# Two attention heads' scores strictly in turns, their values in fp32 on 64-column halves, and ln1_g loaded in one tile with x

## The chip, the cores and the metric

One core of one Trainium2 chip runs the kernel. The metric is the device time of one execution in microseconds (us). The kernel before took 611.07 us (median of 3 runs, 610.78 to 611.39).

## What is computed

One layer of a hybrid decoder on 256 tokens of width 1024, all in float32. The reference, cut to what the change touches:

```python
h  = rms_norm(x, ln1_g)
q, k, v, z, xbc, dt_raw, gate_a, gate_b = split(h @ w_in, IN_OFFSETS)
qh = rms_norm(split_heads(q), q_norm_g)          # 16 heads of 64
kh = rms_norm(split_heads(k), k_norm_g)
s_own = where(kpos <= qpos, qh @ kh.T * 64 ** -0.5, -inf)
att   = softmax(s_own) @ split_heads(v)
y_a = att @ w_o_attn
y_b = mamba2_mixer(z, xbc, dt_raw, ...) @ w_o_ssm
x = x + (sigmoid(gate_a) * y_a + sigmoid(gate_b) * y_b) @ w_out
x = x + SwiGLU(rms_norm(x)) ;  x = x + (p @ w_ple_proj) * sigmoid(rms_norm(x) @ w_ple_gate)
```

With 256 tokens there is one block, so attention is plain causal attention.

## The kernel before

Every large product runs as 128x512 matmuls with activations as weights (one tile of 128 tokens) and the weight matrix as the moving side. To keep float32 accuracy at the speed of the one-pass type fp32r, each operand is split into a rounded high part and the low rest, and three products are summed: high x high, high x low, low x high (`mm3`, L169; `Panel.step`, L319). The weights come from HBM on SP's queue in pieces (`raw`); ScalarE (ACT) rounds a piece (`wh`), VectorE (DVE) subtracts (`wl`) in `split_w` (L230). 2256 of these big matmuls run one after another, in an order that dependencies fix (`queue`, L154: each instruction of TensorE (PE) follows the last big one recorded before it).

Everything else on PE is a small unit between two big matmuls: transposes (L175), the state-space products, attention. These are generators that a small planner (`Filler`, L78) resumes after each big matmul's three products; `fill.now` counts PE's time by a cost per matmul (L167), and the table `LAG` (L68) says how long after one step a task's next may be placed. The framework's scheduler then orders the units that lie behind the same big matmul, and may put some big ones between the members of a unit.

Attention (`attention_task`, L721) takes eight pairs of heads; a pair's 128 features lie on the 128 partitions, one head on each half. `scores` (L725) runs `mm3` for the first head, twice (128 queries on 128 keys, then 128 on 256), and then for the second: twelve fp32r matmuls with 64 rows, into one PSUM tile a head. DVE adds the mask and takes the maximum (L739, L742), ACT exponentiates, DVE normalises (L755). `transp` (L759) transposes the probabilities, six times, and ACT and DVE split them into `h0, l0, h1, l1`. `values` (L777) multiplies v's high and low parts, 128 columns that hold both heads, by both heads' probabilities in six matmuls of 512 and 256 columns; half of each product (one head's v with the other's probabilities) is not used, and the rest is copied out a head at a time (L791, L792). A matmul on fp32 operands, as `transpose` and the state-space `out_` (L637) have it, is two records in the trace.

The start: `load_first` (L250) issues g1 (ln1_g) and x's first tile on ACT's queue and the weight pieces of the first two panels on SP's; `split_h` (L292) multiplies x by g1 on ACT and makes the low part on DVE. Nine matmuls on zeros run before them (L187).

Of the kernel before, what the change touches and what calls it, by code (L numbers as in the profile page):

```python
# [16 lines left out]
P = 128  # L17
T = 256
# [50 lines left out]
    "dt": 9538, "dt.t": 3583, "dt.e": 24762, "dt.low": 1745, "dt.end": 5569, "xbc": 3815, "xbc.t": 1612,  # L69
    "xbc.end": 7699, "z": 8310, "z.t": 1286, "z.end": 1974, "qk": 14749, "qk.t": 2429, "qk.end": 663,  # L70
    "v": 3190, "cb": 436, "rows": 3738, "prep": 3559, "seg": 921, "seg.next": 7841, "out": 9793,
    "out.xdt": 3087, "out.end": 0, "off": 4613, "off.end": 0, "finish": 6096, "finish.ones": 2544, "sc": 857,
    "sc.tr": 2402, "tr": 822, "tr.val": 5876, "val": 3318, "val.end": 8813, "m": 5271, "res": 4539, "ff": 232,
    "ff.end": 5364,
# [34 lines left out]
def tile_layer(ctx: ExitStack, tc: tile.TileContext, xt, xk, pt, vec, w_dt, w_big, w_dn2, w_pp, out):  # L109
# [34 lines left out]

    def bcast(ap2, n):
        return ap2.unsqueeze(2).to_broadcast([ap2.shape[0], ap2.shape[1], n])
# [7 lines left out]
    def queue(ins, main):  # L154


        if fill.last is not None:
            tc.add_manual_dep(
                ins, fill.last.name, mybir.DependencyInfo(mybir.DependencyClass.NoSync, mybir.DependencyReason.DATA),
                reason="order of the tensor engine")  # L160
        if main:
            fill.last = ins

    def mm(o, lhsT, rhs, start, stop, main=False):
        queue(nc.tensor.matmul(o, lhsT, rhs, start=start, stop=stop).ins, main)  # L165
        passes = 4 if lhsT.dtype == F32 else 1
        fill.now += passes * max(107.0, rhs.free_size() / 2.4)  # L167

# [10 lines left out]
    with prio("w"):  # L179
# [7 lines left out]
        for _ in range(9):  # L187
            nc.tensor.matmul(pw[:, :P], zero, zero, start=True, stop=True)
# [31 lines left out]
    def load_x(k, n, queue=nc.sync):  # L220
        queue.dma_start(xraw[k // 2][:, k % 2 : k % 2 + n], xt[:, k : k + n])
# [70 lines left out]
    def split_h(k):  # L292
        g = g1[:, k : k + 1]
        xk_ = xraw[k // 2][:, k % 2]
# [156 lines left out]
    xsT, zsT, bc, qk_t, v_hl, gates = {}, {}, {}, {}, {}, {}  # L451
# [90 lines left out]
    def evac_v(i, pan):  # L542
        vh = s4([2, 512], F32R)
        vl = s4([2, 512], F32R)
        with prio("ev"):
            for tt in range(2):
                act(vh[:, tt], pan.ps[tt], scale=rstd1[:, tt : tt + 1])
                stt(vl[:, tt], pan.ps[tt], rstd1[:, tt : tt + 1], vh[:, tt].bitcast(F32), op0=ALU.mult, op1=ALU.subtract)
        yield fill.now + LAG["v"]
        v_hl[i] = (vh, vl)  # L550
# [13 lines left out]
    def ssm_task():  # L564
# [72 lines left out]
        def out_(g, qd):  # L637
# [3 lines left out]
            with prio("bg"):  # L641
                yds = [pb([2, P]) for _ in range(2)]

                for j in range(2):
                    for c in range(2):
                        for hf in range(2):
                            r0 = slice(64 * hf, 64 * hf + 64)
                            c0 = (2 * qd + j) * P + 64 * hf
                            mm(yds[j][r0, c], xdt[:, c, c0 : c0 + 64], ms[g, qd, c][:, 2 * j + hf], True, True)
# [71 lines left out]
    def attention_task():  # L721
# [3 lines left out]
        def scores(p):  # L725
            half, i = p
            (qh, ql), (kh, kl) = qk_t["q", half], qk_t["k", half]
            with prio("bg"):
                mx = tiny([4])
                sm = tiny([4])  # L730
                sc = []
                s_all = s4([2, 384])
                for hf in range(2):
                    r = slice(64 * hf, 64 * hf + 64)
                    p_ = pb([512])
                    mm3(p_[:, 0:P], qh[r, i, 0:P], ql[r, i, 0:P], kh[r, i, 0:P], kl[r, i, 0:P])
                    mm3(p_[:, P : P + T], qh[r, i, P:T], ql[r, i, P:T], kh[r, i], kl[r, i])
                    s_ = s_all[:, hf]
                    nc.vector.tensor_tensor_reduce(  # L739
                        out=s_[:, 0:P], in0=p_[:, 0:P], in1=cmask[:, 1], scale=1.0, scalar=-3.0e38,  # L740
                        op0=ALU.add, op1=ALU.max, accum_out=mx[:, 2 * hf : 2 * hf + 1])
                    nc.vector.tensor_tensor_reduce(  # L742
                        out=s_[:, P : P + T], in0=p_[:, P : P + T], in1=cmask.rearrange("p a b -> p (a b)"), scale=1.0, scalar=-3.0e38,
                        op0=ALU.add, op1=ALU.max, accum_out=mx[:, 2 * hf + 1 : 2 * hf + 2])
                    sc.append(s_)
                nc.vector.tensor_scalar(mx, mx, -0.125, None, op0=ALU.mult)  # L746
                for hf in range(2):
                    for qt, sl in ((0, slice(0, P)), (1, slice(P, P + T))):
                        n = 2 * hf + qt
                        act(sc[hf][:, sl], sc[hf][:, sl], AF.Exp, scale=0.125, bias=mx[:, n : n + 1], accum_out=sm[:, n : n + 1])  # L750
                nc.vector.reciprocal(sm, sm)
                for hf in range(2):
                    for qt, sl in ((0, slice(0, P)), (1, slice(P, P + T))):
                        n = 2 * hf + qt
                        nc.vector.tensor_scalar(sc[hf][:, sl], sc[hf][:, sl], sm[:, n : n + 1], None, op0=ALU.mult)  # L755
            sc_of[p] = sc
            tm["s", p] = fill.now

        def transp(p):  # L759
            sc = sc_of.pop(p)  # L760
            with prio("bg"):
                p0 = pb([2, T])
                p1 = pb([2, P])
                for hf in range(2):
                    transpose(p0[:, hf, 0:P], sc[hf][:, 0:P])
                    transpose(p0[:, hf, P:T], sc[hf][:, P:T])
                    transpose(p1[:, hf], sc[hf][:, T : T + P])
                hi, lo = s4([6, P], F32R), s4([6, P], F32R)
# [317 lines left out]
```

## Time and profile before

| | us |
|---|---|
| median of 3 runs | 611.07 |
| the profiled execution | 612.0 |
| its span, first to last instruction | 610.2 |
| PE busy | 601.2 (2949 records) |
| DVE busy | 437.8 |
| ACT busy | 341.9 |
| POOL busy | 40.2 |

Busy time of PE is that of overlapping records, so the start of one matmul to the start of the next says more than a record's own length. The mean granted clock of TensorE is given as 0.998 of full rate.

### The profile page before, as it was taken

To read this page: it belongs to the slowest core of one execution; us is meant where nothing else is said; L and a number is where in the kernel's file an instruction comes from. 1 tells how busy PE (TensorE), PEld (TensorE's weight loads), DVE (VectorE), ACT (ScalarE), POOL (GpSimd) and SP (SyncE) were. 2 spreads that over 40 slices of the span, in tenths; PEclk is the share of its full clock that TensorE was granted. 3 is DMA by queue.
4 is the path that set the end of the run, shared out by engine and by line. 5 is a ranking of instruction groups with operands and counts; after the bars stand their busy time and mean duration, and the time that the engine had idled before them with its cause. 6 is when DMAs were issued, how large, how long until landed. Compare 5 with 4: busy or idle time off the path is not lost.

```text
span 610.2 us, 8184 instructions
## 1 busy us (share of the span) xinstructions
PE 601.2 (99%) x2949; PEld 493.1 (81%) x2949; DVE 437.8 (72%) x715; ACT 341.9 (56%) x524; POOL 40.2 (7%) x47
## 2 busy tenths in 40 slices
PE   7999999999999999999999999999999999999997
PEld 6888888777787878888788888888888888888886
DVE  3579999988798774778897576657666666546465
ACT  3676766656584445567647544755544544435353
POOL 2000102331101200102000000000000000000000
PEclk9999999999999999999999999999999999999999
DMA  8755554453435445554444466555556555565641
GB/s 250 259 198 173 182 159 139 145 169 110 139 111 166 156 155 168 168 184 154 139 124 153 146 212 229 172 183 189 180 180 200 173 188 192 176 197 180 195 150 69
DMA packets 31192, 103.88 MB, mean 170 GB/s; under 512 B 3696, under 2 KB 4784, under 8 KB 31152
## 3 DMA queue, kind: packets, MB, share of 16 engines
q1 hardware_dynamic: 30864, 103.23, 52.6%
q8 instruction: 23, 0.38, 0.3%
q10 hardware_dynamic: 288, 0.14, 0.2%
q14 instruction: 17, 0.14, 0.1%
HBM read 102.23 MB, written 1.05 MB: 169 GB/s over the span
## 4 chain that ended last, share of the span: by engine, by line
PE 97%; DMA 1%; DVE 1%; ACT 0%; issue 0%; ACTq 0%
PE g L165 84%; PE pb L165 7%; PE pb L175 5%; DMA xraw<-in_xt 1%; DVE s L474 0%; ACT wh L149 0%; DVE wl L233 0%; ACT s L149 0%; DVE s L526 0%; DVE tiny L522 0%; DVE s L1019 0%; DVE s L1020 0%; ACTq L254 0%; DVE tiny L523 0%; ACT L149 0%
## 5 line engine op out<-in xcount | busy, mean ns | idle before, releaser
L165 PE MATMUL g<-wh,s 128*128 128x512 f32 x1504 | 488.4, 396 | 2.9 <-ACT wh L149 2.9
L165 PEld LDWEIGHTS g<-wh,s 128*128 128x128 f32 x1504 | 283.0, 189 | 62.0 <-ACT wh L149 3.2
L233 DVE TENSOR_TENSOR wl<-raw,wh 128x1024 fp32r<-128x1024 f32 (+1 forms) x192 | 229.8, 1201 | 117.3 <-ACT wh L149 114.8
L165 PE MATMUL g<-wl,s 128*128 128x512 f32 x752 | 295.9, 393 | 0.0
L149 ACT ACTIVATE wh<-raw 128x1024 fp32r<-128x1024 f32 (+1 forms) x192 | 199.4, 1042 | 167.1 <-PE g L165 145.7
L165 PEld LDWEIGHTS g<-wl,s 128*128 128x128 f32 x752 | 142.2, 189 | 27.9 <-DVE wl L233 0.6
L149 ACT ACTIVATE s<-pb 128x512 f32<-128x512 f32 (+5 forms) x76 | 37.2, 505 | 33.9 <-PE pb L175 24.3
L175 PEld LDWEIGHTS pb<-ident,s 128*128 128x128 f32 x302 | 37.8, 140 | 11.5 <-issue 1.2
L175 PE MATMUL pb<-ident,s 128*128 128x128 f32 x302 | 46.7, 272 | 0.0
L149 ACT ACTIVATE s<-g,rstd 128x512 f32<-128x512 f32 (+2 forms) x50 | 28.5, 583 | 22.4 <-PE g L165 21.8
L165 PE MATMUL pb<-s,s 128*64 128x128 f32 (+7 forms) x312 | 39.5, 304 | 0.6 <-DVE s L474 0.6
L165 PEld LDWEIGHTS pb<-s,s 128*64 128x64 f32 (+3 forms) x312 | 30.4, 163 | 9.0 <-issue 4.1
L474 DVE SCALAR_TENSOR_TENSOR s<-pb,vecs,s 128x255 f32<-128x255 f32 (+2 forms) x72 | 32.1, 474 | 1.3 <-ACT s L149 1.1
L149 ACT ACTIVATE s<-pb,vecs 128x256 f32<-128x256 f32 (+2 forms) x48 | 26.0, 552 | 11.8 <-PE pb L175 7.4
L149 ACT ACTIVATE s<-s 128x512 f32<-128x512 f32 (+3 forms) x24 | 19.1, 795 | 8.4 <-DVE s L934 4.0
L335 POOL TENSOR_TENSOR rstd<-tiny,mhalf 128x2 f32<-128x2 f32 x3 | 2.3, 763 | 325.8 <-DVE tiny L334 299.4
L591 POOL TENSOR_SCALAR_AFFINE_SELECT rr<-a_h 128x512 fp32r<-128x512 f32 x16 | 14.3, 902 | 104.3 <-PE pb L165 66.8
L525 POOL TENSOR_TENSOR tiny<-tiny,mhalf 128x8 f32<-128x8 f32 x8 | 15.7, 1966 | 61.1 <-ACT s L149 31.5
L149 ACT ACTIVATE s<-s,tiny 128x128 f32<-128x128 f32 (+1 forms) x32 | 14.1, 446 | 7.0 <-DVE tiny L746 7.0
L978 DVE SCALAR_TENSOR_TENSOR s<-g,rstd,s 128x256 f32<-128x256 f32 x22 | 10.6, 481 | 7.4 <-ACT s L149 7.3
L632 DVE TENSOR_TENSOR s<-s,s 128x512 f32<-128x512 f32 x16 | 11.5, 722 | 0.0
L979 DVE SCALAR_TENSOR_TENSOR s<-g,rstd,s 128x256 f32<-128x256 f32 x22 | 10.6, 484 | 0.8
(121 smaller groups left out, 253.8 us busy)
## 6 DMA issues: line engine op xcount, KB each, us to landing
raw<-in_w_big SPq DMA_DIRECT2D x180, 512.0 KB
raw<-in_w_big SPq DMA_DIRECT2D x8, 256.0 KB
s<-in_xk SPq DMA_DIRECT2D x4, 512.0 KB
raw<-in_w_pp SPq DMA_DIRECT2D x2, 512.0 KB
raw<-in_w_dn SPq DMA_DIRECT2D x2, 512.0 KB
out<-s SPq DMA_DIRECT2D x3, 256.0 KB
xraw<-in_xt SPq DMA_DIRECT2D x2, 256.0 KB
xraw<-in_xt SPq DMA_DIRECT2D x3, 128.0 KB
```

The costliest lines, as they stand in the source:

```text
L149: return nc.scalar.activation(o, i, f, **kw)
L165: queue(nc.tensor.matmul(o, lhsT, rhs, start=start, stop=stop).ins, main)
L175: queue(nc.tensor.transpose(o, i, ident[: i.shape[0], : i.shape[0]]).ins, False)
L233: nc.vector.tensor_sub(wl, raw, wh.bitcast(F32))
L335: nc.gpsimd.tensor_tensor(dst, t, mhalf[:, : ss.shape[-1]], op=ALU.pow)
L474: stt(cc[:, sft:], pu[:, j, : T - sft], cw[3 - sft], cc[:, sft:], op0=ALU.mult, op1=ALU.add)
L525: nc.gpsimd.tensor_tensor(f, ms, mhalf, op=ALU.pow)
L591: nc.gpsimd.affine_select(r, bcast(a_h[:, c, h0 : h0 + 4].bitcast(F32), P), pattern=[[0, 4], [1, P]], compare_op=ALU.is_ge, fill=0.0, base ...
L632: nc.vector.tensor_tensor(m, m, cbm[:, g, c].unsqueeze(1).to_broadcast([P, 4, P]), op=ALU.mult)
L978: stt(t[:, tt], pan.ps[tt][:, :T], r, t[:, tt], op0=ALU.mult, op1=ALU.mult)
L979: stt(t[:, tt], pan.ps[tt][:, T:], r, t[:, tt], op0=ALU.mult, op1=ALU.mult)
```

## The change

- `scores`: the twelve matmuls alternate strictly between the two heads; a new helper, `halves`, chains them so that the scheduler keeps that order. The state-space `out_` is written with the same helper. The normalisation is two broadcast multiplications in place of four.
- `evac_v`, `transp`, `values`: v and the transposed probabilities stay fp32 (no low parts). `values` serves two pairs at a time, in one PSUM tile: each head's product has its own 64 columns of weights and is an fp32 matmul; the heads alternate; one copy on ACT and one subtraction on DVE for both pairs.
- The start: g1 and x's first tile are one array in HBM and one DMA, `x0`, first on SP's queue; seven matmuls on zeros in place of nine.
- The `LAG` table has other numbers, which moves units between other big matmuls.

```diff
 LAG = {
-    "dt": 9538, "dt.t": 3583, "dt.e": 24762, "dt.low": 1745, "dt.end": 5569, "xbc": 3815, "xbc.t": 1612,
+    "dt": 9198, "dt.t": 3823, "dt.e": 24762, "dt.low": 2074, "dt.end": 6965, "xbc": 3815, "xbc.t": 1507,
...
+    def halves(products):
+
+        last = None
+        for a in products:
+            ins = mm(*a)
+            fill.now -= 53.0
+            if last is not None:
+                follow(ins, last)
+            last = ins
...
-        for _ in range(9):
+        for _ in range(7):
...
-    g1 = const.tile([P, 8], F32, name="g1")
+
+    x0 = const.tile([P, 8 + T], F32, name="x0")
+    g1 = x0[:, 0:8]
...
-            nc.scalar.dma_start(g1, vec[:, V_G1 : V_G1 + 8])
-            load_x(0, 1, nc.scalar)
+            nc.sync.dma_start(x0, xt[:, : 8 + T])
...
-        vh = s4([2, 512], F32R)
-        vl = s4([2, 512], F32R)
+        vt = s4([2, 512])
         with prio("ev"):
             for tt in range(2):
-                act(vh[:, tt], pan.ps[tt], scale=rstd1[:, tt : tt + 1])
-                stt(vl[:, tt], pan.ps[tt], rstd1[:, tt : tt + 1], vh[:, tt].bitcast(F32), op0=ALU.mult, op1=ALU.subtract)
+                act(vt[:, tt], pan.ps[tt], scale=rstd1[:, tt : tt + 1])
...
-                    mm3(p_[:, 0:P], qh[r, i, 0:P], ql[r, i, 0:P], kh[r, i, 0:P], kl[r, i, 0:P])
-                    mm3(p_[:, P : P + T], qh[r, i, P:T], ql[r, i, P:T], kh[r, i], kl[r, i])
...
+                halves(
+                    (ps[hf][:, o], a[rows_of[hf], i, qs], b[rows_of[hf], i, ks], n == 0, n == 2)
+                    for o, qs, ks in ((slice(0, P), slice(0, P), slice(0, P)), (slice(P, P + T), slice(P, T), slice(0, T)))
+                    for n, (a, b) in enumerate(((qh, kh), (qh, kl), (ql, kh)))
+                    for hf in range(2))
...
-                act(h0, p0)
-                nc.vector.tensor_sub(l0, p0, h0.bitcast(F32))
-                act(h1, p1)
-                nc.vector.tensor_sub(l1, p1, h1.bitcast(F32))
...
+                act(t0, p0)
+                act(t1, p1)
...
-                mm3(pa, vh[:, 0, cs], vl[:, 0, cs], h0, l0, stop=False)
-                mm3(pa[:, :, P:T], vh[:, 1, cs], vl[:, 1, cs], h1, l1, start=False)
-                for hf in range(2):
-                    r = slice(64 * hf, 64 * hf + 64)
-                    act(ah[r, i], pa[r, hf])
-                    nc.vector.tensor_sub(al[r, i], pa[r, hf], ah[r, i].bitcast(F32))
+                prods = []
+                for i in range(2):
+                    t0, t1 = pr_of.pop((half, i0 + i))
+                    cols = [slice((i0 + i) * P + 64 * hf, (i0 + i) * P + 64 * hf + 64) for hf in range(2)]
+                    prods += [(pa[rows_of[hf], i], vt[:, 0, cols[hf]], t0[:, hf], True, False) for hf in range(2)]
+                    prods += [(pa[rows_of[hf], i, P:T], vt[:, 1, cols[hf]], t1[:, hf], False, True) for hf in range(2)]
+                halves(prods)
+                act(ah, pa)
+                nc.vector.tensor_sub(al, pa, ah.bitcast(F32))
```

A unit of scores on PE before (pb_1532 and pb_1541 are the two heads' PSUM tiles, in each row the moving operand stands first, then the weights: s_188 and s_189 are k's high and low parts, s_222 and s_223 q's):

```order
L165 MATMUL pb_1532<-s_188_1053,s_222_1182 128x128
L165 MATMUL pb_1532<-s_189_1054,s_222_1182 128x128
L165 MATMUL pb_1532<-s_188_1053,s_223_1183 128x128
L165 MATMUL pb_1532<-s_188_1053,s_222_1182 128x256
L165 MATMUL pb_1532<-s_189_1054,s_222_1182 128x256
L165 MATMUL pb_1532<-s_188_1053,s_223_1183 128x256
L165 MATMUL pb_1541<-s_188_1053,s_222_1182 128x128
L165 MATMUL pb_1541<-s_189_1054,s_222_1182 128x128
L165 MATMUL pb_1541<-s_188_1053,s_223_1183 128x128
L165 MATMUL pb_1541<-s_188_1053,s_222_1182 128x256
L165 MATMUL pb_1541<-s_189_1054,s_222_1182 128x256
L165 MATMUL pb_1541<-s_188_1053,s_223_1183 128x256
```

and such a unit in the change, with the heads' tiles pb_1692 and pb_1693:

```order
L170 MATMUL pb_1692<-s_188_1050,s_220_1174 128x128
L170 MATMUL pb_1693<-s_188_1050,s_220_1174 128x128
L170 MATMUL pb_1692<-s_189_1051,s_220_1174 128x128
L170 MATMUL pb_1693<-s_189_1051,s_220_1174 128x128
L170 MATMUL pb_1692<-s_188_1050,s_221_1175 128x128
L170 MATMUL pb_1693<-s_188_1050,s_221_1175 128x128
L170 MATMUL pb_1692<-s_188_1050,s_220_1174 128x256
L170 MATMUL pb_1693<-s_188_1050,s_220_1174 128x256
L170 MATMUL pb_1692<-s_189_1051,s_220_1174 128x256
L170 MATMUL pb_1693<-s_189_1051,s_220_1174 128x256
L170 MATMUL pb_1692<-s_188_1050,s_221_1175 128x256
L170 MATMUL pb_1693<-s_188_1050,s_221_1175 128x256
```

The same twelve products now alternate. Before, six of the eight units stood whole and two had big matmuls between the heads; in the change six stand whole and two have big matmuls after the first of the twelve.

The end of attention on PE before (pb_3409 holds the last pair's values, s_695 and s_696 are the high and low parts of its probabilities, s_583 and s_584 those of v, g_3420 and g_3421 the output projection's panel):

```order
L165 MATMUL pb_3409<-s_695_3372,s_583_2805 128x512
L165 MATMUL g_3421<-wl_3424,s_571_2737 128x512
L165 MATMUL g_3421<-wh_3423,s_572_2738 128x512
L165 MATMUL pb_3409<-s_696_3373,s_583_2805 128x512
L165 MATMUL pb_3409<-s_695_3372,s_584_2806 128x512
L165 MATMUL pb_3409<-s_695_3372,s_583_2805 128x2x128
L165 MATMUL pb_3409<-s_696_3373,s_583_2805 128x2x128
L165 MATMUL pb_3409<-s_695_3372,s_584_2806 128x2x128
L165 MATMUL g_3421<-wh_3423,s_571_2737 128x512
```

and in the change (pb_3316 holds the last two pairs' values, s_687 the last pair's probabilities, s_583 v, both fp32; s_678 and s_679 are the high and low parts that ACT and DVE make of them, the weights of the panel's second half; x2 is the two heads in turn):

```order
L170 MATMUL pb_3316<-s_687_3313,s_583_2796 64x256 x2
L170 MATMUL pb_3316<-s_687_3313,s_583_2796 64x128 x2
L170 MATMUL g_3328<-wh_3336,s_577_2766 128x512
L170 MATMUL g_3327<-wh_3366,s_678_3269 128x512
L170 MATMUL g_3327<-wl_3367,s_678_3269 128x512
L170 MATMUL g_3327<-wh_3366,s_679_3270 128x512
L170 MATMUL g_3327<-wh_3366,s_678_3269 128x512
L170 MATMUL g_3327<-wl_3367,s_678_3269 128x512
L170 MATMUL g_3327<-wh_3366,s_679_3270 128x512
L170 MATMUL g_3327<-wh_3372,s_678_3269 128x512
L170 MATMUL g_3327<-wl_3373,s_678_3269 128x512
L170 MATMUL g_3327<-wh_3372,s_679_3270 128x512
```

The first two rows are the last half of the last values unit, which the order has split; its first half stands 23 big matmuls earlier. Six big matmuls of the second half use features that are long there; the seventh to ninth (wh_3372, the third k step) use those of the last two pairs. Before, the last pair's values stood 15 big matmuls ahead of the panel's second half; now one does.

The start, on ACT before:

```order
L254 DMA g_110<-in_vec 128x8
L149 ACT_TABLE_LOAD
L149 ACTIVATE warm<-warm 128x1
L221 DMA xraw_111<-in_xt 128x256
L149 ACTIVATE s_7_115<-xraw_111,g_110 128x256
L149 ACTIVATE wh_122<-raw_121 128x512
L149 ACTIVATE wh_125<-raw_124 128x512
```

and on SP in the change:

```order
L273 DMA x_108<-in_xt 128x264
L280 DMA raw_118<-in_w_big 128x512
L280 DMA raw_121<-in_w_big 128x512
L240 DMA xraw_109<-in_xt 128x256
L280 DMA raw_118<-in_w_big 128x512
L280 DMA raw_121<-in_w_big 128x512
```

ACT's two DMAs are gone; x and g1 stand ahead of the weight pieces on SP's queue, which were first before.

## Rows read from the trace of the kernel before

**Rows 1.** The page, part 4: the chain that ended last, by engine.
```profile
PE 97%; DMA 1%; DVE 1%; ACT 0%; issue 0%; ACTq 0%
```
**Rows 2.** Timeline of the start, one chain piece among it: start us, length us, what.
```profile
0.80 0.87 SPq L262 DMA_DIRECT2D raw<-in_w_big  x2
1.14 4.21 PE L188 MATMUL pb<-zero 128*128 128x128 f32 x18 [1.14 <-DVE ones L192]
1.29 5.75 DMA xraw<-in_xt
7.13 0.51 ACT L149 ACTIVATE s<-xraw,g 128x256 fp32r<-128x256 f32 x1 [4.40 <-DMA xraw<-in_xt]
8.21 0.80 PE L165 MATMUL g<-wh,s 128*128 128x512 f32 x1 [2.86 <-ACT wh L149]
8.98 1.14 ACT L149 ACTIVATE wh<-raw 128x512 fp32r<-128x512 f32 x2
```
**Rows 3.** Stretches of 2 us: busy us by engine, clock, DMA share, GB/s.
```profile
2.00:4.00 2.00, 2.00 (x11) 2.00 (x11) 0.00 (x0) 0.72 (x2) 1.94 (x8) 1.00 0.87 227
4.00:6.00 2.00, 1.35 (x7) 1.05 (x5) 0.00 (x0) 0.00 (x0) 0.17 (x1) 1.00 0.83 139
```
**Rows 4.** Timeline of PE around 14 us; between two of these rows lie three steps.
```profile
12.94 0.63 PE L165 MATMUL g<-wl,s 128*128 128x512 f32 x1
...
14.20 0.39 PE L165 MATMUL g<-wl,s 128*128 128x512 f32 x1
...
14.90 0.39 PE L165 MATMUL g<-wl,s 128*128 128x512 f32 x1
```
**Rows 5.** Timeline of PE: a whole unit of scores between big matmuls.
```profile
148.28 0.39 PE L165 MATMUL g<-wh,s 128*128 128x512 f32 x1
148.60 1.24 PE L165 MATMUL pb<-s,s 64*128 64x128 f32 x12
149.77 0.50 PE L165 MATMUL g<-wh,s 128*128 128x512 f32 x1
150.11 0.39 PE L165 MATMUL g<-wl,s 128*128 128x512 f32 x1
```
**Rows 6.** Timeline of PE: one head's half of a unit that was split.
```profile
292.22 0.39 PE L165 MATMUL g<-wh,s 128*128 128x512 f32 x1
292.53 0.95 PE L165 MATMUL pb<-s,s 64*128 64x128 f32 x6
293.42 0.50 PE L165 MATMUL g<-wh,s 128*128 128x512 f32 x1
```
**Rows 7.** Timeline of PE: half of a state-space output unit, and a whole one.
```profile
123.18 0.66 PE L165 MATMUL pb<-s,s 128*64 128x128 f32 x8
123.77 0.50 PE L165 MATMUL g<-wl,s 128*128 128x512 f32 x1
...
145.00 0.39 PE L165 MATMUL g<-wh,s 128*128 128x512 f32 x1
145.31 1.09 PE L165 MATMUL pb<-s,s 128*64 128x128 f32 x16
146.34 0.50 PE L165 MATMUL g<-wh,s 128*128 128x512 f32 x1
```
**Rows 8.** Timeline of PE: a unit of values.
```profile
311.10 0.39 PE L165 MATMUL g<-wh,s 128*128 128x512 f32 x1
311.33 1.20 PE L165 MATMUL pb<-s,s 128*128 128x512 f32 x6
312.36 0.40 PE L165 MATMUL g<-wh,s 128*128 128x512 f32 x1
```
**Rows 9.** A wait of PE; ACT and DVE on 128x512: lines, and min/median/max ns.
```profile
PE pb L165 <- DVE s L474: 0.6, 1, 0.6
...
L149 ACT ACTIVATE s<-pb 128x512 f32<-128x512 f32 (+5 forms) x76 | 37.2, 505 | 33.9 <-PE pb L175 24.3
...
L914 DVE TENSOR_TENSOR s<-s,s x4: 682/684/691, 353.0 to 369.5; 128x512 f32<-128x512 f32 x4
```

More of the change, by code (lines that the diff above doesn't have):

```diff
@@ L157, in queue, with follow @@
         if fill.last is not None:
-            tc.add_manual_dep(
-                ins, fill.last.name, mybir.DependencyInfo(mybir.DependencyClass.NoSync, mybir.DependencyReason.DATA),
-                reason="order of the tensor engine")
+            follow(ins, fill.last)
         if main:
             fill.last = ins
+    def follow(ins, before):
+        tc.add_manual_dep(
+            ins, before.name, mybir.DependencyInfo(mybir.DependencyClass.NoSync, mybir.DependencyReason.DATA),
+            reason="order of the tensor engine")
     def mm(o, lhsT, rhs, start, stop, main=False):
-        queue(nc.tensor.matmul(o, lhsT, rhs, start=start, stop=stop).ins, main)
+        ins = nc.tensor.matmul(o, lhsT, rhs, start=start, stop=stop).ins
+        queue(ins, main)
         passes = 4 if lhsT.dtype == F32 else 1
         fill.now += passes * max(107.0, rhs.free_size() / 2.4)
+        return ins
+    def halves(products):
[6 more added lines that the diff above has]
+            last = ins
     def mm3(o, lh, ll, rh, rl, start=True, stop=True):
@@ L293, in split_h @@
         g = g1[:, k : k + 1]
[L294 removed]
+        xk_ = xraw[k // 2][:, k % 2] if k else x0[:, 8:]
         tc.keep_in_program_order(act(h_act[k][0], xk_, scale=g))
@@ L751, in scores @@
                 nc.vector.reciprocal(sm, sm)
[L752 to L756, printed above, removed]
+                for qt, sl in enumerate(parts):
+                    nc.vector.tensor_tensor(
+                        s[:, :, sl], s[:, :, sl], bcast(sm.rearrange("p (h q) -> p h q", h=2)[:, :, qt], sl.stop - sl.start), op=ALU.mult)
@@ L775, in transp, with values @@
+            pr_of[p] = (t0, t1)
             tm["t", p] = fill.now
-        def values(p):
-            half, i = p
-            vh, vl = v_hl[half]
-            if i == 0:
+        def values(half, i0):
+            vt = v_of[half]
+            if i0 == 0:
                 att_hl[half] = (s4([4, T], F32R), s4([4, T], F32R))
-            ah, al = att_hl[half]
-            h0, l0, h1, l1 = pr_of.pop(p)
+            ah, al = (a[:, i0 : i0 + 2] for a in att_hl[half])
             with prio("bg"):
@@ L804, in attention_task @@
                 yield fill.now + LAG["tr"]
-            if 0 <= n - 2 < 8:
+            if n >= 3 and n % 2:
                 p = pairs[n - 2]
-                while p[0] not in v_hl:
+                while p[0] not in v_of:
                     yield fill.now + 500
                 yield tm["t", p] + LAG["tr.val"]
-                values(p)
+                values(p[0], p[1] - 1)
                 yield fill.now + LAG["val"]
```

64 lines of the change are left out of this document (30 added, 34 removed).

## The prediction

> **What bounds the kernel now.** I read the page first: the chain that ended last runs through TensorE (PE) for 97% of the span [rows 1]. So a microsecond counts if it is taken from PE's own sequence or from the time before that sequence starts; work on VectorE (DVE) and ScalarE (ACT) counts only where PE waits for it. The list of PE's waits has one of 2.9 us at the start [rows 2] and one other, of 0.6 us, for a convolution's result [rows 9]. Next I read the timeline of the start: nine warm-up matmuls end at 5.35, PE then stands until 8.21, and what it waits for is x, issued on ACT's queue at 1.29 and used at 7.13, then the rounded weights [rows 2]. Last I read the timeline of PE around each kind of small work that the change touches [rows 5 to 8]. There the useful number is not the busy time, which overlaps, but the price of a unit: from the start of the big matmul before it to the start of the big one after it, less one ordinary step. An ordinary step of a 128x512 matmul is 0.23 us after 14.2 us (0.70 for three) and 0.42 before (1.26 for three) [rows 4]: 512 columns in 0.42 us is the 1.2 GHz level, in 0.23 us close to the 2.4 GHz level. (The clock column of the stretches says 1.00 before 14.2 too [rows 3]; I go by the steps.)
>
> **The start.** Removed are two DMAs on ACT's queue (g1 of 32 bytes a row, then x behind it); the eight columns of g1 and the first 256 of x come as one tile, first on SP's queue, ahead of the first two weight pieces. ACT then does the same three things in the same order: x times g1, the rounded weights, the next rounded weights. Between ACT's start on x and PE's first real matmul lie 8.21 - 7.13 = 1.08 us [rows 2], and they stay. What moves is when x and the first weight piece are there. They are 135 KB and 262 KB, 0.40 MB together. In the kernel before, the DMAs moved 227 GB/s, 0.45 MB, between 2 and 4 us [rows 3], so at that rate the 0.40 MB are through at 3.8 and PE could start at 4.9 and later; how long after its last byte a transfer releases its reader is not in a row, and I add 0.4. Start: 5.3, **gain 2.9**. Bounds: PE can't start before its seven warm-ups end, 1.14 + 7/9 of 4.21 = 4.4 (gain 3.8); if x lands as long after its issue as now (5.75 us [rows 2]) but is issued at 0.80, the gain is 0.5. The two removed warm-ups cost and bring nothing by themselves, since PE waits after them. Each SP piece behind x is issued one DMA (0.43 us) later; the cover is that the second k step is needed only after twelve big matmuls of 0.42 us, at about 10.4, and ACT has that step's two pieces rounded at 10.12 even with the arrivals of the kernel before [rows 2]. How long PE stays at 1.2 GHz I take as now: 8.21 to 14.2, 6 us. Bounds: if the clock were up at once this would give 6.0 x (1 - 0.23/0.42) = 2.7 us more; a rise 2 us later would cost 0.9.
>
> **Scores, eight units of twelve matmuls.** Six units stood whole: 149.77 - 148.28 - 0.23 = 1.26 us, and the first big matmul after them takes 0.34 instead of 0.23 [rows 5], so 1.37. In two units the order has big matmuls between the heads; a half alone costs 293.42 - 292.22 - 0.23 = 0.97 [rows 6], with the exit 1.08. Before: 6 x 1.37 + 4 x 1.08 = 12.5 us. These rows also show that six more matmuls added only 0.29 us: the heads use different halves of the rows, and the second already runs under the first. In strict turns both heads should run side by side from the first matmul, as the pairs of the state-space outputs do on column halves: sixteen records in the time of eight [rows 7]. Then twelve cost what six cost, 0.97, at most a hundredth more: 1.09 with the exit. In the new order two units are split 1 + 11; the lone matmul pays an entry and an exit again, some 0.4 us (0.97 less five steps of 0.11 to 0.17 leaves 0.3, and the exit 0.11). After: 8 x 1.09 + 2 x 0.4 = 9.5. **Gain 3.0.** Bounds: 0.8 if a whole unit stays at 1.26, which merges only the two that were apart; 3.8 if the splits cost nothing.
>
> The Trainium skill ("TensorE: Matmul & The Clock Gate", Part 3, The mechanism) says that matmuls start and end strictly in program order, with only weight loads pulled ahead. By that rule the twelve of a six-and-six unit would run one behind another, the unit would cost about 0.97 + 6 x 0.11 = 1.64, and turns would save 0.38 more in each of six units, 5.3 instead of 3.0. The row has 1.26, so the trace disagrees, and the sum goes by the row.
>
> **Values.** Before: eight units of six fp32r matmuls over 128 columns of weights, 312.36 - 311.10 - 0.23 = 1.03 us, no slower exit [rows 8]; 8.3 us, and some 0.2 more where transposes precede them. After: four units of sixteen products' halves in fp32, that is per unit four turns of 256 columns and four of 128, two heads side by side. The nearest row is the state-space output, also fp32 on 64-column halves: eight products of 128 columns, sixteen records, take 146.34 - 145.00 - 0.23 = 1.11. From first record to next big matmul sixteen take 1.03 and eight 0.59 [rows 7], so four products, two pairs, cost 0.44 and a pair 0.22; of the 1.11, 0.88 is the pairs and 0.23 entry and exit, 0.34 with the slow step behind [rows 5]. I take twice a pair's 0.22 for one of 256 columns, as its columns are twice as many, so a unit has 2 x 0.44 + 2 x 0.22 = 1.32 us, and four units 5.3. The order splits the last one, so five entries: 5 x 0.34 = 1.7. After: 7.0. **Gain 1.5**, since the 64-column halves no longer compute the products of one head's values with the other's probabilities. Bounds: if halves of 256 columns did not run side by side, 5.3 more (a loss of 3.8); if entries cost half, 0.9 better. I take the near row.
>
> **Nearly nothing.** One state-space output unit that was split in two stands whole: 0.34 us less. On DVE and ACT the low parts of probabilities and of v go, the four normalisations become two, the copies out of PSUM are done for two pairs at once: less work, but PE waits for neither in this stretch, so I count 0. The LAG table moves transposes and decay products between big matmuls; their number is the same, and a transpose costs the same anywhere. The place to look at is the end of attention, where the values of the last two pairs now stand one big matmul ahead of the panel's second half. From them ACT makes the high part (0.51 us) and DVE the low part (0.68 [rows 9]), about 1.2 us with nothing else in the way, and what is queued behind them is weight splitting; PE needs the high part seven big matmuls later (1.6 us) and the low part nine later (2.1). It fits by under a microsecond: 0, at most 1.5.
>
> **Sum.** 2.9 + 3.0 + 1.5 + 0.34 = 7.7 us. The profiled execution took 612.0 us, 1.8 of it outside its span, so 604.3; the runs' median is 611.07, 0.9 under it, and against that the forecast is **603.3 us**. With its own bounds (start 4.4 to 6.3, clock, splits) the likeliest case reaches from 601 to 605.
>
> **Rivals.**
> 1. *The start doesn't move.* x lands late for a reason other than sharing: start 7.7, gain 0.5, **605.7**. For it: the DMAs moved less between 4 and 6 us than before, with x still to come [rows 3]; against it: g1's small rows are gone, and x no longer waits behind them. Chance 0.14.
> 2. *Turns bring nothing over what the array overlaps already*: units stay at 1.26, 2.2 us lost, **605.5**. For it: the overlap of 0.97 to 0.29 shows the array finding pairs itself; against: the column halves in turns start in pairs. Chance 0.12.
> 3. *New waits*: scores, transposes and values stand closer together, and PE waits 1 to 1.5 us at the end of attention or at two or three other places, **605 to 606**. Against: the distances counted above. Chance 0.12.
> 4. *Slower: the clock.* PE starts on the first data and then gets it in pieces, so that it stays at 1.2 GHz for longer. Each us there loses 1 - 0.23/0.42 = 0.45 us. The 7.7 us are used up when full rate comes 17 us later than forecast, at about 28 us instead of 11; at 35 us the kernel takes **614**. For it: before 8.21 the rows have nine warm-ups without a rise; against: once PE ran steadily it rose within 6 us. Chance 0.03. The Trainium skill (same page, Part 1) says that activity releases the throttle, idling brings it back and the moment varies from run to run; no row here shows a fall.
>
> **Numbers.** The forecast has 0.59. A difference under 0.2% (1.2 us) could not be told from no change. The first three rivals are all faster by over 5 us alone, and by 1.5 us or so if all three meet; same 0.03, slower 0.03, faster 0.94. The range takes in rivals 1 to 3 singly and the likeliest case's early end: 600.8 to 606.6.
>
> **What would show it.** The first g matmul near 5.3, the 0.42 us steps for about 6 us; whole score units of 1.0 us; values units near 1.55, with the exit step 1.66, with records starting in pairs; no PE wait above 1 us after the start. Wrong would be: a first matmul after 7, score units of 1.26, values units over 2.5, or 0.42 us steps after 15 us.

## The result, and the profile after

The changed kernel took 604.24 us (median of 4 runs, 603.23 to 604.38), the kernel before beside it 611.23 (4 runs, 610.78 to 612.12): ratio 0.988, interval 0.9863 to 0.9897. The forecast was 603.3 us, 600.8 to 606.6. The profiled execution is the fastest of the four, 603.23 us, against 612.0 of the profiled one before: 8.8 us between the two traces, where the medians differ by 7.0.

The page, parts 1 and 4 (busy us, share of the span, count; then the chain that ended last by engine):

```profile
span 601.5 us, 8135 instructions
...
PE 593.8 (99%) x2961; PEld 483.6 (80%) x2961; DVE 423.9 (70%) x667; ACT 338.6 (56%) x512; POOL 38.7 (6%) x47
...
PE 95%; DMA 2%; DVE 2%; ACT 1%; issue 0%; SPq 0%; ACTq 0%; DVEq 0%
```

PE is still what the chain runs through [rows 1]. It is busy 99% of the span, so the waits are few. The list of PE's waits (us in total, times, longest):

```profile
PE g L170 <- ACT wh L151: 1.1, 1, 1.1
...
PE pb L170 <- ACT s L151: 0.4, 1, 0.4
PE pb L170 <- DVE s L716: 0.3, 1, 0.3
```

The 2.9 us for the first rounded weights [rows 2] are 1.1 now; behind the start no wait is over 0.4 us. The timeline of the start (start us, length us, what, in brackets what it waited for); the last row is the first small unit, behind 96 big matmuls:

```profile
3.15 0.51 ACT L151 ACTIVATE s<-x 128x256 fp32r<-128x256 f32 x1 [0.87 <-DMA x<-in_xt]
...
4.90 0.63 ACT L151 ACTIVATE wh<-raw 128x512 fp32r<-128x512 f32 x1 [1.24 <-DMA raw<-in_w_big]
...
5.58 0.50 PE L170 MATMUL g<-wh,s 128*128 128x512 f32 x1 [1.09 <-ACT wh L151]
...
6.31 0.50 PE L170 MATMUL g<-wl,s 128*128 128x512 f32 x1 [0.22 <-DVE wl L252]
...
6.64 0.61 PE L170 MATMUL g<-wh,s 128*128 128x512 f32 x2
...
7.10 0.39 PE L170 MATMUL g<-wl,s 128*128 128x512 f32 x1
...
28.76 2.03 PE L170 MATMUL pb<-s,s 128*64 128x256 f32 x16
```

The same first small unit in the kernel before:

```profile
33.05 2.04 PE L165 MATMUL pb<-s,s 128*64 128x256 f32 x16
```

x is used at 3.15 instead of 7.13, and the first big matmul starts at 5.58 instead of 8.21 [rows 2]. ACT now stands for the first weight piece, not for x. From 6.64 a step is 0.23 us (two in 7.10 - 6.64), the 2.4 GHz level, where the kernel before had 0.42 up to 14 us [rows 4]. The lengths of the records say that this level was there at the first big matmul already: 0.50 us at 5.58, as behind a small unit later on (306.83), but 0.80 at 8.21 before [rows 2]. The clock column says 1.00 all through the start in both traces, so this is read from steps and records; where the column does say 0.50, in an experiment below, a step is 0.43 as well.

From the first small unit to the end of the span, where the start plays no part any more, the kernel before took 577.15 us (610.2 - 33.05) and the change 572.74 (601.5 - 28.76): 4.4 us less.

The timeline of PE around a whole unit of scores, one of values, and an output unit of the state space:

```profile
305.62 0.39 PE L170 MATMUL g<-wh,s 128*128 128x512 f32 x1
305.94 0.96 PE L170 MATMUL pb<-s,s 64*128 64x128 f32 x12
306.83 0.50 PE L170 MATMUL g<-wh,s 128*128 128x512 f32 x1
...
300.55 0.39 PE L170 MATMUL g<-wh,s 128*128 128x512 f32 x1
300.87 1.52 PE L170 MATMUL pb<-s,s 128*64 128x256 f32 x16
302.32 0.50 PE L170 MATMUL g<-wh,s 128*128 128x512 f32 x1
...
108.50 0.39 PE L170 MATMUL g<-wh,s 128*128 128x512 f32 x1
109.25 1.15 PE L170 MATMUL pb<-s,s 128*64 128x128 f32 x16 [0.36 <-ACT s L151]
110.35 0.50 PE L170 MATMUL g<-wh,s 128*128 128x512 f32 x1
```

By the prediction's own price (big start to big start, less 0.23): scores 306.83 - 305.62 - 0.23 = 0.98, before 1.26 [rows 5]; values 302.32 - 300.55 - 0.23 = 1.54; the output unit 110.35 - 108.50 - 0.23 = 1.62 where a whole one was 1.11 [rows 7]; 0.36 of the 0.51 more is a wait for ACT.

### The profile page after: what moved, and what is told of

Read it like the earlier page. It is cut to its first block, busy times and chain, and to the rows that moved or that the text cites. A ratio compares the mean times of both kernels' runs of the same rounds, so it can differ in the third digit from the quotient of the medians.

```text
span 601.5 us, 8135 instructions
## 1 busy us (share of the span) xinstructions
PE 593.8 (99%) x2961; PEld 483.6 (80%) x2961; DVE 423.9 (70%) x667; ACT 338.6 (56%) x512; POOL 38.7 (6%) x47
## 4 chain that ended last, share of the span: by engine, by line
PE 95%; DMA 2%; DVE 2%; ACT 1%; issue 0%; SPq 0%; ACTq 0%; DVEq 0%
PE g L170 83%; PE pb L170 6%; PE pb L192 5%; DMA raw<-in_w_big 2%; DVE wl L252 1%; ACT wh L151 0%; DVE s L722 0%; DVE s L630 0%; ACT s L151 0%; DVE s L757 0%; DVE s L635 0%; DVE s L714 0%; DVE s L314 0%; DVE s L1032 0%; DVE s L1033 0%
## 5 line engine op out<-in xcount | busy, mean ns | idle before, releaser
L170 PE MATMUL g<-wh,s 128*128 128x512 f32 x1504 | 486.5, 395 | 1.1 <-ACT wh L151 1.1
L170 PEld LDWEIGHTS g<-wh,s 128*128 128x128 f32 x1504 | 281.8, 188 | 60.1 <-issue 1.8
L170 PE MATMUL g<-wl,s 128*128 128x512 f32 x752 | 294.8, 392 | 0.4 <-DVE wl L252 0.4
L170 PEld LDWEIGHTS g<-wl,s 128*128 128x128 f32 x752 | 141.5, 188 | 29.1 <-DVE wl L252 1.8
L151 ACT ACTIVATE s<-pb 128x512 f32<-128x512 f32 (+4 forms) x64 | 33.7, 545 | 30.6 <-PE pb L192 16.1
L151 ACT ACTIVATE s<-g,rstd 128x512 f32<-128x512 f32 (+1 forms) x50 | 28.6, 583 | 20.9 <-PE g L170 19.1
L170 PE MATMUL pb<-s,s 128*64 128x128 f32 (+6 forms) x328 | 32.6, 304 | 0.4 <-ACT s L151 0.4
L170 PEld LDWEIGHTS pb<-s,s 128*64 128x64 f32 (+2 forms) x328 | 23.1, 154 | 9.9 <-issue 4.7
L991 DVE SCALAR_TENSOR_TENSOR s<-g,rstd,s 128x256 f32<-128x256 f32 x22 | 10.6, 481 | 7.5 <-ACT s L151 7.5
L992 DVE SCALAR_TENSOR_TENSOR s<-g,rstd,s 128x256 f32<-128x256 f32 x22 | 10.6, 484 | 0.8
```

The source lines that it names most:

```text
L151: return nc.scalar.activation(o, i, f, **kw)
L170: ins = nc.tensor.matmul(o, lhsT, rhs, start=start, stop=stop).ins
L991: stt(t[:, tt], pan.ps[tt][:, :T], r, t[:, tt], op0=ALU.mult, op1=ALU.mult)
L992: stt(t[:, tt], pan.ps[tt][:, T:], r, t[:, tt], op0=ALU.mult, op1=ALU.mult)
```

## The experiments

Theory: three separate gains (start, scores in turns, values), each on PE's path, with a LAG table that only moves units and weighs nothing. Rivals: the gains depend on the table; turns give nothing over six and six; the clock's rise makes the start's gain.

**One part alone in the kernel before.** First the start:

```diff
-            nc.scalar.dma_start(g1, vec[:, V_G1 : V_G1 + 8])
-            load_x(0, 1, nc.scalar)
+            nc.sync.dma_start(x0, xt[:, : 8 + T])
...
-        for _ in range(9):
+        for _ in range(7):
```

> The kernel before with the new start alone: x and ln1_g in one tile first on SP's queue, seven warm-up matmuls. Theory A (the start pays by itself and in two parts: 2.6 us from an earlier first matmul, up to 2.8 us from a clock that is at full rate sooner): first big matmul near 5.6 us, time 2.6 to 5.4 us under the kernel before (605.8 to 608.6). Theory B (what the start gains is given back while the first panels wait for data): first big matmul near 5.6 but under 1 us gained, over 610.

608.38 us, ratio 0.9957 [0.9944, 0.9970]: 2.6 us faster (1.8 to 3.4), as theory A has it. Its first big matmul:

```profile
6.05 0.80 PE L165 MATMUL g<-wh,s 128*128 128x512 f32 x1 [1.55 <-ACT wh L149]
```

This is 2.2 us earlier than in the kernel before. From there to the first small unit it took 23.5 us (29.55 - 6.05) for 24.8, as the steps were 0.23 from 9.4 on; so the clock gave 1.3 of the 3.5 us between the two spans (610.2 and 606.7). The total lies near the forecast's 2.9, but a part of it is clock, for which the forecast had nothing. Behind the first small unit the two traces agree (577.15 us in both).

Then the turns, with the table of before:

```diff
-                    mm3(p_[:, 0:P], qh[r, i, 0:P], ql[r, i, 0:P], kh[r, i, 0:P], kl[r, i, 0:P])
-                    mm3(p_[:, P : P + T], qh[r, i, P:T], ql[r, i, P:T], kh[r, i], kl[r, i])
...
+                halves(
+                    (ps[hf][:, o], a[rows_of[hf], i, qs], b[rows_of[hf], i, ks], n == 0, n == 2)
...
+                    for hf in range(2))
```

> The kernel before with the strict turns of the scores alone (its own LAG table; three of the eight units are split after the first matmul). Theory A (twelve matmuls in turns cost what six cost): whole units of 0.97 to 1.0 us before the exit step, 2.6 us gained (3.0, less one more split), about 608.6. Theory B (the array overlaps the two heads as well by itself): whole units of 1.26, at most 0.8 us gained, 610.4 or more.

611.05 us, ratio 0.9996 [0.9987, 1.0005]: nothing. But the units did get shorter. The timeline of PE in that kernel, a unit of scores and, later, a wait that the kernel before does not have:

```profile
147.81 0.39 PE L170 MATMUL g<-wh,s 128*128 128x512 f32 x1
148.12 0.96 PE L170 MATMUL pb<-s,s 64*128 64x128 f32 x12
149.01 0.50 PE L170 MATMUL g<-wh,s 128*128 128x512 f32 x1
...
178.21 0.74 PE L170 MATMUL g<-wh,s 128*128 128x512 f32 x2 [1.07 <-DVE s L725]
```

The unit costs 149.01 - 147.81 - 0.23 = 0.97. PE then waits 1.07 us for the low part that DVE makes at the end of the state space (L725). More units were also torn: three of scores into 1 + 11, each lone matmul about 0.35 us, and two more output units into halves. From the first small unit on, this trace took 576.85 us (609.4 - 32.55), the kernel before 577.15, so the start is not what hides a gain. Theory A is right on the units and wrong on the time: the wait and the two output units (0.34 each by the forecast's price) take back 1.75 of its 2.6 us, and the rest was not traced. Shorter units change the planner's count, and with it where all that follows is put.

Last the values:

```diff
-                mm3(pa, vh[:, 0, cs], vl[:, 0, cs], h0, l0, stop=False)
-                mm3(pa[:, :, P:T], vh[:, 1, cs], vl[:, 1, cs], h1, l1, start=False)
...
+                halves(prods)
```

> The kernel before with the values in fp32 on 64-column halves alone, two pairs at once (its own LAG table; no unit of values is split in the order, two of scores are, as before). Theory A (a unit is 1.55 us before the exit step and replaces two of 1.03): 1.8 us gained, about 609.4. Theory B (the four passes of fp32 cost more than the unused half did): units over 2 us, no gain or a loss, 611 or more.

609.88 us, ratio 0.9975 [0.9966, 0.9984]: 1.5 us faster (1.0 to 2.1). Units cost 1.54 to 1.55 us, and there is no new wait. The three together make some 4.4 us of the 7.3 that the interval of the change centres on; about 3 are left that no part alone gave.

**The table taken back.** The changed kernel with the LAG numbers of before:

```diff
-    "dt": 9198, "dt.t": 3823, "dt.e": 24762, "dt.low": 2074, "dt.end": 6965, "xbc": 3815, "xbc.t": 1507,
+    "dt": 9538, "dt.t": 3583, "dt.e": 24762, "dt.low": 1745, "dt.end": 5569, "xbc": 3815, "xbc.t": 1612,
...
```

> The changed kernel with the LAG table of the kernel before. Theory A (the table only moves units, and what it is worth is the splits it avoids, four of 0.4 us here against three): 0 to 1 us slower than the changed kernel, 604.2 to 605.2. Theory B (the new table takes away waits of TensorE and so carries a part of the gain): 606 or more, with waits of TensorE over 1 us in its profile.

613.43 us, ratio 1.0037 [1.0023, 1.0051]: 9.2 us more than the change, and slower than the kernel before. The timeline of PE, in an execution of 615.35 us:

```profile
172.40 0.95 PE L170 MATMUL pb<-s,s 64*128 64x128 f32 x12
179.09 0.45 PE L192 MATMUL pb<-ident,s 128*128 128x128 f32 x1 [5.74 <-DVE s L768]
...
181.78 1.65 PE L170 MATMUL pb<-s,s 64*128 64x128 f32 x12
...
185.13 0.63 PE L170 MATMUL g<-wh,s 128*128 128x512 f32 x1
185.56 0.63 PE L170 MATMUL g<-wl,s 128*128 128x512 f32 x1
```

Transposes stand directly behind a unit of scores, and PE waits 5.74 us for a normalisation (L768). What follows runs at half the rate: the same twelve products take 1.65 instead of 0.95 us, a step 0.43 (185.56 - 185.13), the 1.2 GHz level. The stretches of 4 us (length, then busy us of PE, weight loads, DVE, ACT and POOL with their counts, granted clock, DMA share, GB/s) show the fall:

```profile
174.00:178.00 4.00, 0.00 (x0) 0.00 (x0) 4.00 (x13) 1.11 (x3) 0.00 (x0) 0.74 0.40 131
178.00:182.00 4.00, 2.75 (x12) 2.19 (x14) 2.87 (x8) 3.04 (x11) 0.00 (x0) 0.50 0.39 131
182.00:186.00 4.00, 4.00 (x21) 3.14 (x21) 3.08 (x12) 4.00 (x10) 0.59 (x1) 0.50 0.00 0
186.00:190.00 4.00, 3.81 (x19) 3.05 (x19) 3.63 (x10) 2.36 (x9) 0.90 (x2) 0.98 0.00 1
```

The fall that no row of the kernel before had is here: the clock goes to half while PE stands, and stays there until 186. That agrees with the Trainium skill ("TensorE: Matmul & The Clock Gate", Part 1), by which idling brings the throttle back. Behind the wait's end lie some 7 us at half rate, which cost about 3 (an estimate: 7 x (1 - 0.23/0.43)). With the wait's 5.7 that is 9 of the 10.0 us that this trace is longer than the change's from the first small unit on (613.6 - 30.82 = 582.8).

**Which numbers of the table?** Once the six for attention from the new table and all others old, once a single one (the numbers alone are shown):

```diff
-    "sc": 857, "sc.tr": 2402, "tr": 822, "tr.val": 5876, "val": 3318, "val.end": 8813,
+    "sc": 6834, "sc.tr": 2218, "tr": 0, "tr.val": 759, "val": 2876, "val.end": 3654,
...
-    "sc": 857,
+    "sc": 6834,
```

> The changed kernel with the LAG table of before, except for its six attention numbers (sc, sc.tr, tr, tr.val, val, val.end), which are the new ones. The changed kernel took 604.2 us, the changed kernel with the whole old table 613.4. Theory A: the old table fails by its attention numbers alone, because with them two score units stand directly ahead of their own transposes (5.7 us of wait and 10 us at half the clock behind it); then this one takes 604.0 to 606.0 us, with no wait of PE over 1.5 us and the granted clock full from the start's rise to the end. Theory B: the state-space numbers carry as much, since the old ones made PE wait for ssm_finish in the kernel that had only the turns; then 607 us or more, with that wait in the list of waits. No part of the computation is changed.

> The changed kernel with the LAG table of before, but for one number: sc (the stretch of PE work that the planner keeps free behind a scores unit) is 6834 as in the new table instead of 857. Theory A: this one number is what moves the transposes away from the scores that they need; it takes back the 5.7 us wait and the half clock, 5.7 + 5.1 = 10.8 us of the 613.4 us, so 602.6, and with the lone split units and entries of the old order (about 1 to 2 us) 603.5 to 605.5 us. Theory B: the clock falls for another reason than that wait, or the wait only moves to the next transposes: 608 us or more. Theory C: the other five attention numbers matter too: over 1 us slower than the run with all six of the new ones. No part of the computation is changed.

612.65 us, ratio 1.0025 [1.0016, 1.0034], and 614.18, ratio 1.0042 [1.0030, 1.0055]. Theory A is wrong in both: the 5.74 us wait is gone, but the time is not. Of the first run theory B holds, over 607 us with a wait for the end of the state space. Between the two lie 1.5 us, with intervals that meet, so whether the other five attention numbers matter stays open. PE with the six numbers, around the same place (this kernel's lines are five lower, L165 is L170 and L717 is L722):

```profile
172.20 0.95 PE L165 MATMUL pb<-s,s 64*128 64x128 f32 x11 [1.02 <-ACT s L146]
...
174.96 0.50 PE L165 MATMUL g<-wh,s 128*128 128x512 f32 x1 [1.38 <-ACT s L146]
...
177.60 1.22 PE L165 MATMUL g<-wh,s 128*128 128x512 f32 x2 [1.92 <-DVE s L717]
```

One long wait has become three of 1.0 to 1.9 us, for ACT and for DVE's end of the state space (L717); with the single number they are 1.0, 1.4 and 1.4. The stretches of the first kernel show what stands around them:

```profile
162.00:166.00 4.00, 4.00 (x19) 2.45 (x18) 1.83 (x2) 1.35 (x3) 0.00 (x0) 1.00 0.69 219
...
170.00:174.00 4.00, 2.56 (x22) 1.80 (x20) 4.00 (x7) 4.00 (x10) 0.35 (x1) 1.00 0.27 83
174.00:178.00 4.00, 1.13 (x3) 0.69 (x4) 4.00 (x15) 2.58 (x6) 0.57 (x1) 0.71 0.52 180
178.00:182.00 4.00, 4.00 (x10) 3.07 (x10) 2.95 (x8) 1.86 (x8) 0.00 (x0) 0.50 0.00 0
182.00:186.00 4.00, 4.00 (x22) 3.19 (x22) 1.02 (x1) 1.81 (x2) 0.09 (x1) 0.93 0.00 0
```

DVE is busy 1.83 of 4 us in the first of these, 8 of 8 from 170 to 178 while PE works 3.69 of 8, and 1.02 of 4 in the last. The work is the same; the old table bunches it, and the wait sits with whoever comes last. The clock fell at about 175.7, as the third wait began (granted 0.86 from 175 to 176, 0.50 in the next us); from 171 to 176 PE had worked 2.28 of 5 us. In the changed kernel the same part is spread:

```profile
165.00:169.00 4.00, 4.00 (x21) 3.25 (x21) 4.00 (x14) 4.00 (x8) 0.00 (x0) 1.00 0.51 176
169.00:173.00 4.00, 3.66 (x29) 2.89 (x29) 4.00 (x8) 4.00 (x12) 1.49 (x2) 1.00 0.01 4
```

DVE and ACT are full here too, 8 of 8 us, but PE works 7.66 of 8, and DVE had 3.44 of 4 in the stretch before (161 to 165), where the other kernel had 1.83. So PE bounds the kernel as a whole, but in this part DVE and ACT are as full, and PE stays fed where their work is spread evenly. That this evenness is the whole cause is read from the stretches and was not tested by itself. The numbers for attention alone don't give that order.

**The table alone.** The kernel before with nothing but the new numbers:

```diff
-    "dt": 9538, "dt.t": 3583, "dt.e": 24762, "dt.low": 1745, "dt.end": 5569, "xbc": 3815, "xbc.t": 1612,
+    "dt": 9198, "dt.t": 3823, "dt.e": 24762, "dt.low": 2074, "dt.end": 6965, "xbc": 3815, "xbc.t": 1507,
...
```

> The kernel before with the new LAG table and nothing else. Theory A: a table fits the lengths of the units for which it was made, and here the long units of before fall behind it: at the end of the state-space part the last scores, transposes and values stand close together, the last transposes 5 main products (1.2 us) behind the scores that they need, so PE waits some 3 to 6 us there and may lose the full clock behind it: 614 to 622 us. Theory B: the table orders the work better whatever the units' lengths, and gives about the 2.4 us that the separate gains of start, turns and values leave to it: 608 to 609 us. No part of the computation is changed.

618.31 us, ratio 1.0114 [1.0100, 1.0128]: theory A. At the end of attention its PE has

```profile
350.65 0.50 PE L165 MATMUL g<-wh,s 128*128 128x512 f32 x1 [1.93 <-ACT s L149]
...
357.26 0.50 PE L165 MATMUL g<-wh,s 128*128 128x512 f32 x1 [1.09 <-ACT s L149]
```

though the waits forecast for the transposes did not come; what is late there is ACT's output. Here the granted clock stayed at 1.00. Behind the first small unit its waits are 5.0 us in all, in the kernel before 0.6; it is 7.7 us longer there (616.5 - 31.64 = 584.86 for 577.15), and the rest was not traced. Old units with the old table 611, new units with the old table 613 (with the new start, which alone gave 2.6), old units with the new table 618, both new 604: table and units are one change.

**The order within a unit, under the new table.** Scores six and six, and values one column half after the other:

```diff
+                    for hf in range(2)
...
                     for n, (a, b) in enumerate(((qh, kh), (qh, kl), (ql, kh)))
-                    for hf in range(2))
```

> The changed kernel with each scores unit chained as six matmuls of the first head and then six of the second. Theory A (the turns are what makes the unit short): whole units of 1.26 us against 0.98, 8 x 0.28 = 2.2 us slower than the changed kernel, a little more for units split between the heads. Theory B (it is the chaining in one block and not the turns): whole units of 1.0, within 0.5 us of the changed kernel.

```diff
-                halves(prods)
+                halves(prods[0::2] + prods[1::2])
```

> The changed kernel with the values unit chained as all products of the first column half and then all of the second. Theory A (only neighbours on different halves run side by side, as far ahead as the array looks): between 1.55 and 2.87 us a unit (0.23 + 2 x 1.32), near 2.2, so 2 to 4 us slower than the changed kernel. Theory B (the array finds the pairs itself whatever the order): units of 1.55, same time.

Each took 606.9 us, ratio 0.9929 ([0.9915, 0.9942] and [0.9917, 0.9942]), 2.7 us more than the change. A unit of scores in the first, a unit of values in the second:

```profile
308.81 0.39 PE L170 MATMUL g<-wh,s 128*128 128x512 f32 x1
309.13 1.24 PE L170 MATMUL pb<-s,s 64*128 64x128 f32 x12
310.29 0.50 PE L170 MATMUL g<-wh,s 128*128 128x512 f32 x1
```

```profile
301.77 0.39 PE L170 MATMUL g<-wh,s 128*128 128x512 f32 x1
302.09 2.22 PE L170 MATMUL pb<-s,s 128*64 128x256 f32 x16
304.24 0.50 PE L170 MATMUL g<-wh,s 128*128 128x512 f32 x1
```

Scores cost 310.29 - 308.81 - 0.23 = 1.25 us again: 0.27 more in six units, and two are torn between the heads, at some 0.6 more each (2 x 0.97 for 0.97 + 0.35), 2.9 together. Values cost 304.24 - 301.77 - 0.23 = 2.24, 0.70 more in four units, 2.8. Turns are worth this on both kinds, where the order around them fits. From the first small unit on, these traces took 575.33 and 575.43 us, the change 572.74, so the 2.7 us are not the start's.

The starts of single matmuls show how. In the change the twelve of a scores unit start in six pairs, the two of a pair within 0.01 us (305.94, 306.11, 306.22, 306.33, 306.50, 306.62). Six and six, the second head is not held back until the first is done: the fourth matmul to start (309.41) has 128 columns and the first of 256 starts at 309.51, though in program order the fourth to sixth are the first head's three of 256. But before 309.40 the first head is alone, and the last two (309.97, 310.09) again have no partner. So the overlap of six and six is real and partial, and turns complete it.

**The clock at the start.** Nine warm-ups, and one, in place of seven:

```diff
-        for _ in range(7):
+        for _ in range(9):
...
-        for _ in range(7):
+        for _ in range(1):
```

> The changed kernel with nine warm-up matmuls again (they end near 5.4 at half rate, just under the first matmul at 5.6). Theory A (the clock's rise comes after a stretch of steady work, and two more warm-ups close most of the pause of 1.1 us before the first big matmul): full rate at the first big matmul in every look, same time or up to 1 us faster than the changed kernel. Theory B (the number of warm-ups changes nothing but when they end): same time within 0.3 us.

> The changed kernel with one warm-up matmul in place of seven. Theory A (without the warm-ups the first big matmuls run at half rate for about as long as they did in the kernel before, 14 steps of 0.42 us instead of 0.23): first big matmul still near 5.6, 0.42 us steps behind it, 1.5 to 3 us slower than the changed kernel. Theory B (the clock rises by itself at that time, or data keeps the first steps slow anyway): under 0.5 us slower.

603.13 us (ratio 0.9872 [0.9858, 0.9887]) and 605.02 (0.9898 [0.9884, 0.9911]); both intervals meet that of the change. With nine, theory A's sign did not come: the records of the first two big matmuls are still 0.80 us long, and the level rose near 7. With one, 0.8 us more than the change is what neither theory has. There the steps stay at the lower level to about 10.7 us; this is its PE, the last row being its first small unit:

```profile
9.07 0.63 PE L170 MATMUL g<-wl,s 128*128 128x512 f32 x1
9.50 1.05 PE L170 MATMUL g<-wh,s 128*128 128x512 f32 x2
...
10.74 0.62 PE L170 MATMUL g<-wh,s 128*128 128x512 f32 x2
11.20 0.39 PE L170 MATMUL g<-wl,s 128*128 128x512 f32 x1
...
30.04 2.03 PE L170 MATMUL pb<-s,s 128*64 128x256 f32 x16
```

From the first big matmul to the first small unit are 23.2 us in the changed kernel (28.76 - 5.58), and 24.4 here (30.04 - 5.62): five us at half rate cost 1.2, and not the 2.3 of 5.1 x (1 - 0.23/0.42), as PE at full rate waits for rounded weights in this stretch (96 steps of 0.23 are 22.1). Behind it the traces with one, seven and nine agree to 0.1 us (572.76, 572.74, 572.80). The kernel with six and six has the change's start and seven warm-ups, and still rose only near 10.5, and that with the old table near 12.2: the moment differs between executions.

**A later transpose.** The changed kernel with nine warm-ups, and a number that was to put transposes later behind their scores:

```diff
-    "sc.tr": 2218,
+    "sc.tr": 2641,
...
-        for _ in range(7):
+        for _ in range(9):
```

> The changed kernel with 9 warm-up products instead of 7 and sc.tr 2641 instead of 2218: the transposes of a unit come a little later behind its scores, PE is entered 6 times less between main products (120 instead of 126 times), and two out units lose what stood between their halves. If an entry is worth what a lone one costs beyond its own products (0.1 to 0.2 us), this gives 0.6 to 1.2 us: 602.0 to 603.6 us against 604.2 for the changed kernel and 603.1 for it with 9 warm-ups. The rival is that the entries cost nothing beyond their own products and the time stays at 603.1 to 604.2; a third, that the later transposes delay a values unit and a new wait of 1 us or more shows: 604.5 or more. No part of the computation is changed.

603.11 us (0.9869 [0.9856, 0.9883]), as with nine warm-ups alone. But in its trace all matmuls of PE behind the warm-ups stand in the same order as in the change, by operand names and shapes: the six entries fewer are not there. So the run does not say what an entry costs; it is the nine warm-ups measured again. No version here beats the change by more than the intervals.

## Why the prediction was right, and where not

- **Start**, forecast 2.9: the first big matmul came 2.63 us earlier, at 5.58 for 5.3. Right. The mechanism differs in one point: x is in use at 3.15, where the forecast has ACT on it at 4.2, and the first weight piece decides (ACT at 4.90). The part alone gave 2.6 as well, but out of 2.2 of start and 1.3 of clock in its trace.
- **Clock**, taken as before, 6 us at the lower level: this term fell. In the profiled execution it was up at the first big matmul, which is the forecast's own bound of 2.7 us more. From the first big matmul to the first small unit it took 23.2 us (28.76 - 5.58), before 24.8 (33.05 - 8.21), 1.7 us gained; the bound was not reached because of the waits for weights. In traces of other kernels with this start it rose as late as 12.2. The four runs' median lies 1 us above the profiled one, which is about what the clock is worth; that it is the cause was not shown.
- **Scores**, units 0.97 and gain 3.0: units 0.98; taking the turns back costs 2.7. Right, under the new table.
- **Values**, units 1.55 and gain 1.5: units 1.54; 1.5 alone. Right.
- **Behind the start** the two traces differ by 4.4 us (577.15 and 572.74), where the forecast had 3.0 + 1.5 + 0.34 = 4.8.
- **Output unit**, 0.34 us gained: not found; no output unit is split now, but the one at 109 waits 0.36 us for ACT, and costs 0.5 more than a whole one did.
- **"The LAG table moves transposes ... their number is the same, and a transpose costs the same anywhere"**: this step fell. As a term against the kernel before it came to nothing, as counted, and the end of attention, which it singled out, held no wait. But the zero is a sum: without the new numbers PE would have lost some 9 us. I counted units and not their distances to DVE's and ACT's work, and took DVE and ACT as out of the way because PE did not wait for them in the kernel before. That the new table fits the new units nothing in the working had shown, so on this term the forecast was lucky.
- **The total**: 7.0 us between the medians for a forecast of 7.7, but 8.8 between the traces, with 1.7 of clock in it that the forecast did not count. The terms behind it, 2.6 and 4.4, fell short of theirs by 0.3 and 0.4.
- **Rivals**: 1 (start) and 2 (turns bring nothing) fell. 3 (new waits) is what the old table would have given, far beyond its 1 to 1.5 us; in the change the waits behind the start are 0.7 us, in the kernel before 0.6. 4 (clock) named the wrong place: the fall came not at the start but at a standstill in the middle, and not in the change but with the old table.
- **A six-and-six unit with its matmuls one behind another**, 1.64, was rightly set aside for the row's 1.26: the single starts above show the second head beginning out of its turn.

Left open: which state-space numbers matter, since they were not tried without the others; which part of the start counts, the one DMA in place of two or SP's queue in place of ACT's; and what the two broadcast normalisations and `out_` with the helper give, which no run has alone.

## What to carry to other kernels

Where two engines beside the bound are full for a stretch, a shorter unit on the bound engine need not give its time by itself (the turns gave nothing, the values gave theirs): the schedule made for the old lengths may have to be made again, and each should be measured with the other. Two streams of small products on different halves of the array did best in strict turns, in both kinds of unit here; read a unit's price from big matmul to big matmul, not from busy time. A test of one part under the old schedule can say "nothing" of a part that is worth 2.7 us. And look into the trace whether an edit moved what it was to move, before its time is read.

## What was not expected of the hardware

A standstill of PE of 5.7 us cost some 3 us more behind it: the granted clock was at half until 186 us, some 7 us past the end of the wait. Shorter waits, of 1.0 and 1.4 us close together, brought the same fall, which came as a third of 1.9 us began; the waits of 1.9 and 1.1 us in the old kernel with the new table did not. The moment at which the clock rises at the start differs by several us between executions with the same start: before 5.6, at 10.6 and at 12.2 in three traces. And of twelve matmuls chained six and six, the second head's on the other half of the rows started ahead of their place in the program (309.41, before the first head's of 256 columns at 309.51).
